# The first two blocks of an input projection computed by token halves, two of its columns moved into an earlier pool, and a third pair of split tiles

## The chip, the cores and the metric

The kernel runs on one core of one Trainium2 chip. The metric is device microseconds of that core for one execution of the whole layer. TensorE (PE) does the matrix products, VectorE (DVE), ScalarE (ACT) and GpSimd (POOL) the elementwise work, SyncE (SP) issues the transfers of the hardware queue. Each engine takes its own instructions strictly in the order in which they were put there; an instruction that waits holds up all that stand behind it on that engine.

## The reference, cut to what matters

One layer over 2048 tokens of width 1024, in 32-bit floats, with a memory of 256 tokens.

```python
u = rms_norm(h, g_mix_pre);  z = u @ w_in            # (2048, 2816)
qa, ka, va, qh, fh, ih, gh = split(z)                # 512,128,128,512,512,512,512 columns
ya = swa_with_sinks(qa, ka, va, sinks)               # 8 heads of 64, window of 128, chunks of 64
yh = hgrn2(qh, fh, ih, gh, lb, onorm)                # 4 heads of 128, gated recurrence, chunks of 64
h = h + rms_norm(concat(ya, yh) @ w_out)
m = rms_norm(mem)
h = h + rms_norm(cross_attention(rms_norm(h), m, wq, wk, wv, wo))   # 4 heads, 256 memory tokens
u = rms_norm(h);  h = h + rms_norm((silu(u @ w_gate) * (u @ w_up)) @ w_down)
```

In `hgrn2` the gate is f = lb + (1 - lb) sigmoid(fh), and the recurrence needs sums of log f over a chunk; this is the only logarithm of the layer.

## The kernel before, in words

Every product of two 32-bit numbers is made as three products of a split: a tile is written as a rounded high part and the rest (`split2`: the high part by ACT or POOL, L886 or L888, the low part by DVE as a subtraction, L889), and a matrix product is hi·hi + hi·lo + lo·hi. One such step is 128 rows by 512 columns and stands in the profile as three lines: L1017, L1018 and L1019 in `products`, L156, L157 and L158 in `mm3`.

**Stages on TensorE.** (1) `in_first`, 0 to 260 us: the input projection for the first 1024 tokens, transposed (z columns on the partitions). (2) 260 to 640 us: the same columns for the second 1024 tokens (`in_proj`, `in_cols`, one block of 128 columns at a time, weights through `wcols`), interleaved with sliding-window attention (`swa`) and the recurrence (`hgrn`) of the first half. (3) 640 to 790 us: `hgrn` of the second half, interleaved with `fold_cross`, which folds the cross-attention weights with the 256 memory tokens (products of 256 columns, weights through `wcols`). (4) 790 us to the end: the large products (w_out, cross attention, SwiGLU) as jobs of `phases`.

**Stage 1 in detail.** The order of the columns is `ORDER`: pairs of 128-column blocks, (4, 5) first, then (0, 1), (2, 3), then four pairs (10+h, 6+h) of which 10+h is a forget gate f (an "f block" below), then four pairs of the rest. `phases` runs them as one job. The contraction is cut in two halves of 512, the tokens of stage 1 in two halves of 512. For the first two blocks all eight products of the 2x2x2 cut are made (`eight`; the kinds "q" and "p"); all later ones use seven products of sums (`seven`, kind "s"), which need sums of the token quarters (`T` tiles, made from `raw` in `combined`, L915). The steps of a plain block are called 1, 2 (first token half, both halves of the contraction) and 8, 3 (second token half). In kind "q" the first token half is done in two pieces of 256 tokens.

x arrives in eight tiles of 128 tokens (`x_loads`). Each is normalised (`normed`: sum of squares by ACT at L409 into a `junk` tile, root by POOL at L102 and L104, scaling by DVE at L411), transposed by TensorE (8 transposes of 128x128, L440, in `flipped`), and evacuated: for the first token half by `first` (L457, L458: the split straight from PSUM) and `copied` (L446: the plain copy for the sums), for the second half by `later` (copy, then `split2` on POOL). The remaining eight x tiles, the second 1024 tokens, ride beside the blocks (`beside`): loaded into a `pair` tile, normalised, transposed and stored to DRAM (`un_d`).

`pair` tiles are 128 x 2 x 1024 in five buffers; they hold the z results of a block (`out`), the x tiles beside, and the scratch tile `e` in which the logarithm and the decays of an f block are made (`decays`, L629 the logarithm with a table load before and after). `part` tiles (128x512, three buffers) hold evacuated partial products (L1032) and the tanh of gates (L560). `after` finishes a block while the next is on TensorE: decays, then the two stores of z. PSUM has six banks for products and two for transposes (`psm`, `pss`).

**Around stage 2.** Stage 1 has pools of its own (`t1`, `t2`, `s1`, PSUM `ps1`). When it is over they close, and the pools of stage 2 open over the same memory: `hg` (all tiles of `swa` and `hgrn`), `wp` (three `raw` tiles, two pairs `whi`/`wlo`), `io`. `in_proj(1, u)` first makes columns 4 and 5 together, then the rest one by one. `swa_front` loads its queries `qd`, splits them (L669, L670), and makes the scores at L704 and L705; `hgrn_front` begins with the products of `qq` and `k` at L785.

**What sets the order.** The program is written once, in the order above; a scheduler then places instructions on each engine by a cost of its own, and `yield` points only say which piece is issued after which. The pools' waits are per tile: a tile that lies on an old pool's memory waits for the last use of what lay there.

## Time and profile before

| what | value |
|---|---|
| runs | 2616.89, 2620.36, 2624.73 us (median 2620.36) |
| profiled execution | 2620.68 us, its span 2619.0 us, granted TensorE clock 0.997 |
| TensorE busy | 2549.2 us, 97% |
| DVE, ACT, POOL busy | 1751.4, 1262.2, 435.6 us |
| chain that ended last | PE 75%, DMA 9%, issue 6%, DVE 5%, ACT 3% |

The span is what one execution takes between its first and last instruction in the profile; the 1.7 us around it are in the run's time alone. With TensorE busy 97% of the time, the 70 us in which it is not are the ones to look at, and besides them the microseconds in which it is busy at a lower granted clock. In a row of the timeline, the figure in brackets is how long the engine stood idle before the instruction and which instruction of which line ended that.

### The profile page before, as it was taken

To read this page: it belongs to the slowest core of one execution; us is meant where nothing else is said; L and a number is where in the kernel's file an instruction comes from. 1 tells how busy PE (TensorE), PEld (TensorE's weight loads), DVE (VectorE), ACT (ScalarE), POOL (GpSimd) and SP (SyncE) were. 2 spreads that over 40 slices of the span, in tenths; PEclk is the share of its full clock that TensorE was granted. 3 is DMA by queue.
4 is the path that set the end of the run, shared out by engine and by line. 5 is a ranking of instruction groups with operands and counts; after the bars stand their busy time and mean duration, and the time that the engine had idled before them with its cause. 6 is when DMAs were issued, how large, how long until landed. Compare 5 with 4: busy or idle time off the path is not lost.

```text
span 2619.0 us, 34847 instructions
## 1 busy us (share of the span) xinstructions
PE 2549.2 (97%) x12317; PEld 2132.4 (81%) x12317; DVE 1751.4 (67%) x2757; ACT 1262.2 (48%) x2632; POOL 435.6 (17%) x611
## 2 busy tenths in 40 slices
PE   7999999999999999999999999999999999999998
PEld 6877888888888877888878888888888888888786
DVE  7675578877545778788885655566666556564656
ACT  5463366655555566565563333344333334443543
POOL 4231344321311333212310000000000000000022
PEclk9999999999999999999999999999999999999999
DMA  5345655675877886675974622353565444566888
GB/s 185 126 147 175 190 156 164 196 234 152 246 260 265 303 289 230 216 244 186 307 252 127 205 91 79 105 193 121 177 201 193 153 136 152 201 202 184 254 213 217
DMA packets 364111, 506.03 MB, mean 193 GB/s; under 512 B 20896, under 2 KB 250272, under 8 KB 363936
## 3 DMA queue, kind: packets, MB, share of 16 engines
q1 hardware_dynamic: 357888, 481.77, 56.6%
q0 software_dynamic: 6048, 22.02, 4.7%
q8 instruction: 97, 1.59, 0.3%
q14 instruction: 78, 0.64, 0.1%
HBM read 337.00 MB, written 166.72 MB: 192 GB/s over the span
## 4 chain that ended last, share of the span: by engine, by line
PE 75%; DMA 9%; issue 6%; DVE 5%; ACT 3%; POOL 2%; SPq 1%; DVEq 0%; POOLq 0%; ACTq 0%
PE psm L1017 20%; PE psm L1018 20%; PE psm L1019 20%; PE psg L158 2%; PE psg L157 2%; PE psg L156 2%; DMA row<-y_d 1%; PE pss L1252 1%; DMA z<-in_w_out_dram 1%; DMA u_d<-row 1%; DMA h1t_d<-row 1%; SPq L75 1%; DVE T L889 1%; DMA qq<-z_d 0%; ACT T L886 0%
## 5 line engine op out<-in xcount | busy, mean ns | idle before, releaser
L1017 PE MATMUL psm<-T,S 128*128 128x512 f32 x2695 | 1044.5, 392 | 16.8 <-ACT part L1032 9.8
L1018 PE MATMUL psm<-T,S 128*128 128x512 f32 x2695 | 1049.4, 390 | 2.7 <-DVE T L889 2.6
L1019 PE MATMUL psm<-T,S 128*128 128x512 f32 x2695 | 1038.8, 390 | 4.0 <-DVE S L889 4.0
L1017 PEld LDWEIGHTS psm<-T,S 128*128 128x128 f32 x2695 | 506.7, 188 | 127.4 <-ACT part L1032 10.6
L1019 PEld LDWEIGHTS psm<-T,S 128*128 128x128 f32 x2695 | 506.6, 188 | 110.9 <-DVE S L889 5.7
L1018 PEld LDWEIGHTS psm<-T,S 128*128 128x128 f32 x2695 | 507.0, 188 | 107.8 <-DVE T L889 4.7
L889 DVE TENSOR_TENSOR S<-sraw,S 128x512 fp32r<-128x512 f32 (+1 forms) x319 | 218.2, 690 | 220.2 <-ACT S L886 204.7
L886 ACT ACTIVATE S<-sum 128x512 fp32r<-128x512 f32 (+1 forms) x314 | 188.9, 620 | 361.4 <-PE psm L1019 271.6
L889 DVE TENSOR_TENSOR S<-sum,S 128x512 fp32r<-128x512 f32 (+1 forms) x372 | 249.2, 680 | 50.6 <-ACT S L886 31.7
L1032 ACT ACTIVATE part<-psm 128x512 f32<-128x512 f32 x273 | 161.7, 597 | 247.2 <-PE psm L1019 231.7
L886 ACT ACTIVATE S<-sraw 128x512 fp32r<-128x512 f32 (+1 forms) x272 | 167.3, 616 | 109.4 <-PE psm L1019 99.6
L1378 POOL DMA_DIRECT2D row<-y_d x28 | 26.1, 932 | 1114.3 <-DVE row L1564 1021.0
L889 DVE TENSOR_TENSOR T<-row,T 128x1024 fp32r<-128x1024 f32 (+1 forms) x120 | 140.9, 1188 | 59.5 <-ACT T L886 59.0
L156 PE MATMUL psg<-u,whi 128*128 128x512 f32 x352 | 141.6, 402 | 1.7 <-POOL whi L888 1.7
L158 PE MATMUL psg<-u,wlo 128*128 128x512 f32 x352 | 140.3, 399 | 0.9 <-DVE wlo L889 0.9
L157 PE MATMUL psg<-u,whi 128*128 128x512 f32 x352 | 140.1, 398 | 0.0
L1349 ACT ACTIVATE junk<-row 128x512 f32<-128x512 f32 x160 | 99.8, 625 | 64.7 <-DVE row L1371 31.2
L886 ACT ACTIVATE T<-row 128x1024 fp32r<-128x1024 f32 x120 | 120.1, 1028 | 16.8 <-DMA row<-in_w_down_dram 7.9
L888 POOL TENSOR_SCALAR S<-sum 128x512 fp32r<-128x512 f32 x58 | 54.8, 945 | 297.0 <-PE psm L1019 224.8
L1515 DVE TENSOR_TENSOR row<-psm,part 128x512 f32<-128x512 f32 x66 | 43.7, 687 | 60.6 <-PE psm L1019 60.5
L1524 DVE TENSOR_TENSOR part<-psm,part 128x512 f32<-128x512 f32 x60 | 39.8, 688 | 62.1 <-PE psm L1019 62.0
L156 PEld LDWEIGHTS psg<-u,whi 128*128 128x128 f32 x352 | 66.7, 189 | 14.6 <-POOL whi L888 2.1
(339 smaller groups left out, 3639.3 us busy)
## 6 DMA issues: line engine op xcount, KB each, us to landing
sraw<-in_w_gate_dram SPq DMA_DIRECT2D x44, 512.0 KB, 3.9
sraw<-in_w_up_dram SPq DMA_DIRECT2D x44, 512.0 KB, 3.8
hid_d<-row SPq DMA_DIRECT2D x44, 512.0 KB, 2.6
h_d<-row SPq DMA_DIRECT2D x32, 512.0 KB, 5.2
y_d<-row SPq DMA_DIRECT2D x32, 512.0 KB, 3.4
sraw<-hid_d SPq DMA_DIRECT2D x32, 512.0 KB, 5.5
row<-y_d POOLq DMA_DIRECT2D x28, 512.0 KB, 7.9
sraw<-in_w_in_dram SPq DMA_DIRECT2D x44, 256.0 KB, 3.5
```

The lines of the kernel that those rows point to most:

```text
L156: nc.tensor.matmul(ps, ah, bh, start=(i == 0), stop=False)
L157: nc.tensor.matmul(ps, ah, bl, start=False, stop=False)
L158: nc.tensor.matmul(ps, al, bh, start=False, stop=(i == n - 1))
L886: self.nc.scalar.activation(hi, raw, AF.Copy)
L888: self.nc.gpsimd.tensor_scalar(hi, raw, 1.0, 1.0, ALU.mult, ALU.mult)
L889: self.nc.vector.tensor_tensor(lo, raw, f32(hi), ALU.subtract)
L1017: nc.tensor.matmul(ps, s[:, 0, k, :], t[:, 0, k, :], start=st, stop=False, **kw)
L1018: nc.tensor.matmul(ps, s[:, 0, k, :], t[:, 1, k, :], start=False, stop=False, **kw)
L1019: nc.tensor.matmul(ps, s[:, 1, k, :], t[:, 0, k, :], start=False, stop=sp, **kw)
L1032: nc.scalar.activation(t, ps, AF.Copy)
L1349: self.nc.scalar.activation(junk, a, AF.Square, scale=float(D) ** -0.5, accum_out=to)
L1515: nc.vector.tensor_tensor(d, a, c, ALU.add)
```

## The change

It has three parts, and it moves instructions.

*First two blocks by token halves.* The steps of blocks (4, 5) and (0, 1) are put in another order: first token half of the first block (kind "q"), first token half of the second block (kind "u"), then the second token half of the first and of the second ("v", twice). The second token half of x is so needed two half-blocks later than before. The split weights of both blocks stay in memory that long; those of the second lie in a tile of the T pool (`S_u`). 36 transposes of the identity into an unused bank stand at the start of TensorE's work, and 18 more behind the transposes of the first x tile (`turns`). The orders on ACT, DVE and POOL around the x tiles are fixed by `queued`, the sums of squares use another tile as junk, two of the x loads go behind the weights of the second block, the constants of the mixers (`mix_consts`) go last. z of these two blocks goes through 512-wide `part` tiles with a store each (eight stores of 256 KB in place of four of 512 KB). The loads of x tiles beside are issued in `after` of the block ahead.

*Two columns moved.* Columns 4 and 5 of the second 1024 tokens (96 products of 128x512, L156 to L158) are made at the end of `in_first`, with streamed S tiles and the PSUM banks of stage 1, and not by `in_cols` in stage 2. `in_proj` then begins with the third column.

*Fold.* `fold_cross` uses a third pair of split tiles, every third time; the eight split instructions that open the w_out job are issued in the last half of the `hgrn` loop and not behind it.

The start, on TensorE. `pss` and `psm` are PSUM banks, `x_0` the x tiles of the first token half, `u_00` the split of its first contraction half, `S` the split weights. Before, and then after:

```order
L440 MATMUL pss_145<-ident,x_0_111 128x128 x4
L440 MATMUL pss_150<-ident,x_0_111 128x128 x4
L440 MATMUL psm_166<-ident,x_0_111 128x128 x4
L440 MATMUL psm_171<-ident,x_0_111 128x128 x4
L440 MATMUL psm_199<-ident,x_0_111 128x128 x4
L440 MATMUL psm_204<-ident,x_0_111 128x128 x4
L1017 MATMUL psm_367<-u_00_121,S_180 128x256
```

```order
L444 MATMUL pss_132<-ident 128x128 x36
L475 MATMUL pss_179<-ident,x_0_111 128x128 x4
L475 MATMUL pss_184<-ident,x_0_111 128x128 x4
L444 MATMUL psm_193<-ident 128x128 x18
L475 MATMUL psm_231<-ident,x_0_111 128x128 x4
L475 MATMUL psm_236<-ident,x_0_111 128x128 x4
L1117 MATMUL psm_251<-u_00_120,S_219 128x256
```

The first product stood behind three x tiles and now stands behind two; 54 transposes of the identity are new. Further down, the transposes of the last three of four tiles of the second token half (`x_1`) stood together before, with the first tile beside (`pair_359`) behind them, ahead of the first product on the second half (`u_01`):

```order
L440 MATMUL pss_272<-ident,x_1_133 128x128 x4
L440 MATMUL pss_277<-ident,x_1_133 128x128 x4
L440 MATMUL pss_295<-ident,x_1_133 128x128 x4
L440 MATMUL pss_300<-ident,x_1_133 128x128 x4
L440 MATMUL pss_318<-ident,x_1_133 128x128 x4
L440 MATMUL pss_323<-ident,x_1_133 128x128 x4
L1252 MATMUL pss_794<-ident,pair_359 128x128 x4
L1252 MATMUL pss_800<-ident,pair_359 128x128 x4
L1017 MATMUL psm_479<-u_01_122,S_180 128x512
```

```order
L475 MATMUL pss_423<-ident,x_1_169 128x128 x4
L475 MATMUL pss_428<-ident,x_1_169 128x128 x4
L475 MATMUL psm_446<-ident,x_1_169 128x128 x4
L475 MATMUL psm_451<-ident,x_1_169 128x128 x4
L1117 MATMUL psm_462<-u_00_120,S_u 128x512
L1118 MATMUL psm_462<-u_00_120,S_u 128x512
```

Now two of its tiles stand ahead of the second block's first half (`S_u`), the other two 24 products further on, and the first product on `u_01` comes behind all 48 products of that half-block.

The f blocks, on ACT, around the second logarithm of stage 1 (with the semaphores that each row waits for; DMAHW are transfers). Before, `pair_1124` and `pair_1247` being z and scratch tile of that block, and then after, where these are `pair_1184` and `pair_1307`:

```order
L560 ACTIVATE th_1148<-pair_1124 128x512 [waits DVE_49]
L554 ACTIVATE pair_1124<-pair_1124 128x512 [waits DVE_49]
L629 ACT_TABLE_LOAD [waits DMAHW1_49,DMAHW0_49]
L629 ACTIVATE pair_1247<-pair_1124 128x1024 [waits Pool_49]
L409 ACTIVATE pair_1212,n_s_1606<-pair_1212 128x1024 [waits DMAHW2_49,Activation_49]
L560 ACT_TABLE_LOAD
L560 ACTIVATE th_1204<-psm_1036 128x512 [waits PE_49]
L1032 ACTIVATE part_1233<-psm_1220 128x512
```

```order
L649 ACTIVATE th_1208<-pair_1184 128x512 [waits DVE_49]
L643 ACTIVATE pair_1184<-pair_1184 128x512 [waits DVE_49]
L723 ACT_TABLE_LOAD
L723 ACTIVATE pair_1307<-pair_1184 128x1024 [waits Pool_49]
L649 ACT_TABLE_LOAD
L649 ACTIVATE th_1264<-psm_1094 128x512 [waits PE_49]
L1132 ACTIVATE part_1291<-psm_1278 128x512
```

The logarithm waited for two transfers, the stores of z of the f block ahead of it, whose buffer its scratch tile takes; now it waits for none, and the sum of squares of an x tile beside (L409) has moved from between the table loads to ahead of the block.

The passage from stage 1 to stage 2, on TensorE. `whi` is the first weight tile of the new pools. Before, and then after:

```order
L1018 MATMUL psm_2060<-T_647,S_2157 128x512
L1019 MATMUL psm_2060<-T_647,S_2157 128x512
L156 MATMUL psg_2265<-u_00_2196,whi_2253 128x512
L157 MATMUL psg_2265<-u_00_2196,whi_2253 128x512
...
L157 MATMUL psg_2378<-u_00_2196,whi_2373 128x512
L685 MATMUL pss_2452<-ident,vr_2450 128x128
L704 MATMUL pst_2462<-kh_2445,qs_0_2434 128x128
```

```order
L1118 MATMUL psm_2222<-u_10_122,S_2200 128x512
L1119 MATMUL psm_2222<-u_10_122,S_2200 128x512
L156 MATMUL psm_2295<-u_00_2258,S_2282 128x512
L157 MATMUL psm_2295<-u_00_2258,S_2282 128x512
...
L156 MATMUL psg_2443<-u_00_2258,whi_2438 128x512
...
L879 MATMUL psh_2599<-qq_2592,k_2590 128x192 x2
...
L798 MATMUL pst_2527<-kh_2510,qs_0_2499 128x128
```

The 96 products from the tiles `S_2282` on are now the last of stage 1 and read weights that were loaded in its pools; behind them come 48 products of the first new column, and then the first products of `hgrn` (L879) and `swa` (L798). Before, 96 products and a piece of a third column stood between the new pools' first tile and `swa`.

The diff, cut to its core:

```diff
-                for _ in range(2):
-                    next(cols)
+                next(cols)
...
-                for _ in self.hgrn(range(NPB, NT), "gt"):
+                for i, _ in enumerate(self.hgrn(range(NPB, NT), "gt")):
                     for _ in range(2):
                         next(fold)
-                for _ in range(8):
-                    next(phases)
+                    if 2 <= i < 10:
+                        next(phases)
...
+        turn = itertools.count()
+
+        def split_tiles():
+
+            if next(turn) % 3 < 2:
+                return self.split_tiles()
+            self._n += 1
+            return [ph.tile([P, D], F32R, tag=f"w{x}", name=f"w{x}_{self._n}") for x in ("hi", "lo")]
...
+    def turns(self, kind, n):
+
+        ps = self.bank(kind)
+        for _ in range(n):
+            self.nc.tensor.transpose(ps[:, 0:P], self.ident, self.ident)
...
-        blocks = [("q" if i == 0 else "p" if i < 2 else "s",)
-                  + self.in_block(*p, beside[i], get if i > 9 else (), None if i else lambda: x_loads(0, (2, 3)))
...
+        plain = [b[1:4] + ([],) for b in blocks[:2]]
+        blocks[:2] = ([(k, stream, out, lambda: iter(()), keep) for k, (stream, out, _, keep) in zip("qu", plain)]
+                      + [("v", lambda kind: iter([None]), out, after, keep) for _, out, after, keep in plain])
...
         next(phases)
+        self.turns("h", 36)
+        x_loads(1, (0, 1))
+        scaled(0, 0)
         b0 = first(0, "sh")
+        a0 = self.traced(ACT)
+        with self.queued(self.traced(PE)):
+            self.turns("g", 18)
+        scaled(0, 1)
+        with self.queued(self.traced(POOL), self.traced(DVE)):
+            next(phases)
         b1 = first(1, "gt")
+        a1, v1 = self.traced(ACT), self.traced(DVE)
         next(phases)
+        next(phases)
...
         for i in range(4):
-            later(i)
-        self.mix_consts()
+            if i == 2:
+                next(phases)
+                w = self.traced(PE)
+            with self.queued(*([w] if i > 1 else [])):
+                later(i, a3 if i else a2, v3)
+        self.mark()
+        with self.behind():
+            self.mix_consts()
...
+        c0 = self.ORDER[0][0] * P
+        stream = self.streamed(
+            lambda t, j: self.load(t, I["w_in"][j * 512:(j + 1) * 512, c0:c0 + 2 * P].rearrange("(k p) c -> p k c", p=P)),
+            4, "p")
+        next(stream)
+        S = list(stream)
+        z = self.pair_tile()
+        for s in range(2):
+            for i in range(2):
+                ps = self.bank("g")
+                self.mm3(ps, [((S[i + k // 4 * 2][:, 0, k % 4, :], S[i + k // 4 * 2][:, 1, k % 4, :]), u[s][k])
+                              for k in range(KT)])
+                nc.scalar.activation(z[:, i, s * 512:(s + 1) * 512], ps, AF.Copy)
+        for i in range(2):
+            self.store(self.z_d[c0 + i * P:c0 + (i + 1) * P, TB:2 * TB], z[:, i, :])
...
+                t = self.st_pool.tile([P, 512], F32, tag="part", name=f"zp_{self._n}", bufs=3)
+                nc.scalar.activation(t, a, AF.Copy)
+                self.store(self.z_d[c0:c0 + P, j * 512:(j + 1) * 512], t)
+                return
...
+            for n in beside:
+                t = self.pair_tile()
+                self.load(t[:, 0, :], self.I["x"][TB + n * P:TB + (n + 1) * P, :])
+                ahead.append((n, t))
...
-        for cols in [order[:2]] + [[c] for c in order[2:]]:
-            e1 = self.in_cols(b, u, cols, e1)
+        for c in order[2:]:
+            e1 = self.in_cols(b, u, [c], e1)
...
-    STEPS = {"s": (1, 5, 6, 3, 7, 2, 4), "p": (1, 2, 8, 3), "q": (1, 2, 8, 3)}
-    TAKES = {"s": (1,) * 7, "p": (2, 2, 0, 0), "q": (4, 0, 0, 0)}
+    STEPS = {"s": (1, 5, 6, 3, 7, 2, 4), "p": (1, 2, 8, 3), "q": (1, 2), "u": (1, 2), "v": (8, 3)}
+    TAKES = {"s": (1,) * 7, "p": (2, 2, 0, 0), "q": (4, 0), "u": (2, 2), "v": (0, 0)}
...
+        k1, k2, j = (1, 2, 0) if kind == "u" else (8, 3, 1)
+        if kind == "u":
+            keep += S[:2]
+        self.products(x, [(keep[0], T[k1], nk)], True, False)
+        self.products(y, [(keep[1], T[k1], nk)], True, False)
```

More of the change, by code (lines that the diff above doesn't have):

```diff
@@ L1111, in phases @@
         queue = sorted(uses, key=lambda k: (uses[k][0] - (5 if k[1] == 7 and jobs[k[0]][3] is None else 0), k))
-        slots = [("A", -2, i) for i in range(4)] + [("B", -1, i) for i in range(3)]
+        held = 7 if first else -1
+        slots = [("A", -2, i) for i in range(4)] + [("B", held if i == 2 else -1, i) for i in range(3)]
         T, keep = {}, [{} for _ in jobs]
@@ L1220, in phases @@
                 run = (self.seven(ready, Ready(), nk, out, addend) if kind == "s" else
-                       self.eight(ready, Ready(), nk, out, addend, kind == "q"))
+                       self.eight(ready, Ready(), nk, out) if kind == "p" else
+                       self.plain(ready, Ready(), nk, out, addend, kind))
                 for q in range(len(self.STEPS[kind])):
-                    next(run)
+                    for _ in range(1 if g or not first else 3):
+                        next(run)
+                        if first and g < 3:
+                            yield
                     self.mark()
                     upto(need[g + 2])
+                    if first and g == 1:
+                        yield
                     for _ in range(1 if kind == "s" else 2):
@@ L1234, in phases @@
                             split(g)
-                        half(g, self.row_tile)
+                        if not first or g > 1:
+                            half(g, self.row_tile)
                     g += 1
```

137 lines of the change are left out of this document (86 added, 51 removed).

## The prediction

> **What bounds the kernel now.** I read the page first, then windows of 20 us, then, where a window shows TensorE short of 20 us, the timeline of TensorE and of the engine that its row names.
>
> ```profile
> PE 2549.2 (97%) x12317; PEld 2132.4 (81%) x12317; DVE 1751.4 (67%) x2757; ACT 1262.2 (48%) x2632; POOL 435.6 (17%) x611
> ```
>
> ```profile
> core 0: us, PE busy (x) PEld busy (x) DVE busy (x) ACT busy (x) POOL busy (x), PEclk, DMA share, GB/s
> 0.00:20.00 20.00, 8.54 (x36) 7.45 (x37) 11.39 (x17) 12.86 (x24) 10.43 (x23) 1.00 0.92 303
> 20.00:40.00 20.00, 17.00 (x135) 15.62 (x133) 14.63 (x20) 12.47 (x25) 11.09 (x17) 1.00 0.33 92
> 80.00:100.00 20.00, 20.00 (x90) 16.53 (x89) 10.53 (x15) 5.65 (x11) 2.93 (x5) 1.00 0.45 149
> 140.00:160.00 20.00, 16.89 (x69) 13.81 (x70) 15.79 (x21) 11.42 (x20) 7.00 (x10) 0.91 0.46 144
> 260.00:280.00 20.00, 17.59 (x69) 14.16 (x70) 10.77 (x15) 4.05 (x6) 11.59 (x13) 0.91 0.96 246
> 760.00:780.00 20.00, 16.10 (x129) 15.48 (x130) 13.64 (x19) 9.15 (x14) 1.83 (x3) 1.00 1.03 337
> ```
>
> TensorE is the bound, and in a full window (80 to 100 us) nothing else matters. The change can only win where TensorE is idle or slow: the start, the f blocks (140), the passage (260), the fold (760). The large products after 790 us are the same as before.
>
> **The start.** TensorE, timeline, with the last step of the identity on POOL and one entry of the chain of waits (the splits of the second token half on POOL):
>
> ```profile
> 1.15 0.29 POOL masks.py:199 TENSOR_SCALAR_AFFINE_SELECT ident<-ident 128x128 f32<-128x128 f32 x1
> ```
>
> ```profile
> 35.24 3.16 POOL u L888 x4
> ```
>
> ```profile
> 8.14 1.97 PE L440 MATMUL pss<-ident,x 128*128 128x128 f32 x8 [8.14 <-DVE x L411]
> 12.44 1.97 PE L440 MATMUL psm<-ident,x 128*128 128x128 f32 x8 [2.33 <-DVE x L411]
> 15.39 1.97 PE L440 MATMUL psm<-ident,x 128*128 128x128 f32 x8 [0.98 <-DVE x L411]
> 17.01 0.78 PE L1017 MATMUL psm<-u,S 128*128 128x256 f32 x2
> 20.52 0.41 PE L1018 MATMUL psm<-u,S 128*128 128x256 f32 x1
> 20.73 0.33 PE L1019 MATMUL psm<-u,S 128*128 128x256 f32 x1
> 25.24 0.28 PE L1017 MATMUL psm<-u,S 128*128 128x256 f32 x1
> 25.36 0.28 PE L1018 MATMUL psm<-u,S 128*128 128x256 f32 x1
> 27.43 0.39 PE L1018 MATMUL psm<-u,S 128*128 128x256 f32 x1 [1.43 <-DVE u L458]
> 33.91 1.03 PE L440 MATMUL pss<-ident,x 128*128 128x128 f32 x8
> 39.97 0.98 PE L1017 MATMUL psm<-u,S 128*128 128x512 f32 x3 [0.93 <-POOL u L888]
> 43.09 0.39 PE L1019 MATMUL psm<-u,S 128*128 128x512 f32 x1
> 43.32 0.39 PE L1018 MATMUL psm<-u,S 128*128 128x512 f32 x1
> ```
>
> A product of 256 columns takes 0.21 us up to 20.73 and 0.12 us later; eight transposes 1.97 and then 1.03. TensorE runs at half speed until it has worked without a pause for some 5 us (15.39 to 20.73). A product of 512 columns takes 0.23 us. Before: first product at 17.01; the first block's first half (96 products of 256) ends at 33.9; then TensorE transposes and waits for the second token half until 39.97; then three half-blocks of 48 products of 512, 3 x 10.9 = 32.7 us. The third block starts at 72.7.
>
> After, worked out with the same rows: the identity is there at 1.44, and TensorE can start at about 1.6. 36 transposes, 22 at 0.246 and 14 at 0.129, end at 1.6 + 5.4 + 1.8 = 8.8, 0.7 us behind the first x tile; the next tile cannot be transposed before 12.4 (its DVE row is unchanged), and the 18 further transposes fill that gap. So the first product comes at 12.4 + 1.0 = 13.4, at full speed. 96 products (11.5 us), 16 transposes within (2.1) and one wait like that of 27.43 (1.4) end at 28.4. The second block's first half and the 32 transposes of the second token half (10.9 + 4.1) end at 43.4. The splits of that half on POOL (3.2 us for four, behind the last transposes at about 38) are then just ready. Two half-blocks remain, 21.8: the third block starts at 65.2, against 72.7, less 1.0 for the transposes of a tile beside that stood ahead and come later: **gain 6.5 us**. At worst the transposes of the identity stay slow throughout (36 x 0.246 = 8.9, end at 10.5) and the splits on POOL come 2 us late: 3. At best the wait of 1.4 is gone: 8.
>
> Eight z stores through three `part` buffers cost nothing as I see it: outputs come in pairs 5 to 11 us apart and a store lands within 5.4 (the row below), so three buffers last.
>
> **The f blocks.** The logarithm of the second f block on ACT, the chain ahead of it, and what TensorE waited for:
>
> ```profile
> 131.79 5.39 DMA z_d<-pair
> ```
>
> ```profile
> 137.28 1.28 ACT L629 ACT_TABLE_LOAD   x1 [3.64 <-DMA z_d<-pair]
> ```
>
> ```profile
> 119.71 0.50 PE L1017 MATMUL psm<-T,S 128*128 128x512 f32 x1 [0.55 <-ACT part L1032]
> 143.12 0.50 PE L1017 MATMUL psm<-T,S 128*128 128x512 f32 x1 [3.20 <-ACT part L1032]
> 166.04 0.50 PE L1017 MATMUL psm<-T,S 128*128 128x512 f32 x1 [1.08 <-ACT part L1032]
> ```
>
> ```profile
> 144.00:148.00 4.00, 4.00 (x12) 3.13 (x11) 3.15 (x4) 1.28 (x4) 0.70 (x3) 0.61 0.46 131
> 264.00:268.00 4.00, 4.00 (x13) 3.18 (x13) 4.00 (x3) 0.00 (x0) 3.38 (x4) 0.68 1.16 309
> ```
>
> ACT stands 3.64 us at the table load, for a store; the evacuation of a PSUM bank (L1032) is queued behind it, and TensorE waits 3.20 for that and then runs at a granted clock of 0.61: 12 products in 4 us where 17.5 fit, another 1.3. The order after shows this logarithm waiting for no transfer. What remains is the first f block's case, in which ACT's own chain of two table loads costs 0.55. So (3.20 - 0.55) + (1.08 - 0.55) + 1.3 = **4.5 us**. Bounds: 0 if the scratch tile of another block meets a late store instead, 5.5 if the rest goes too (the sum of squares no longer stands between the table loads).
>
> [...]
>
> **The passage.** TensorE and, for the cover that goes, SP's queue, the transfers from 255 to 290 us (KB each, us from issue to landing) and ACT:
>
> ```profile
> 261.47 0.50 PE L156 MATMUL psg<-u,whi 128*128 128x512 f32 x1 [1.67 <-POOL whi L888]
> 263.14 0.79 PE L158 MATMUL psg<-u,wlo 128*128 128x512 f32 x1 [0.94 <-DVE wlo L889]
> 286.69 0.31 PE L704 MATMUL pst<-kh,qs 128*128 128x128 f32 x1
> ```
>
> ```profile
> 268.03 3.00 SPq L75 DMA_DIRECT2D qd<-z_d  x2
> ```
>
> ```profile
> raw<-in_w_in_dram SPq DMA_DIRECT2D x7, 512.0 KB, 6.5
> qd<-z_d SPq DMA_DIRECT2D x6, 128.0 KB, 3.2
> ```
>
> ```profile
> 276.86 0.64 ACT L669 ACTIVATE qs<-qd 128x512 fp32r<-128x512 f32 x1 [6.17 <-DMA qd<-z_d]
> ```
>
> The first weight tile of the new pools waits for their memory, its load and its split: 1.67 + 0.94 idle and 13 products in 4 us at clock 0.68 (1.4 lost): 4.0 us. The 96 moved products (21.9 us) read weights that were loaded earlier, and the new pools' weights load and are split under them, so these 4.0 go. But the same 96 products were the cover for `swa` and `hgrn`: `qs` was ready 18 us after stage 1's end (259.8, which is 261.47 less 1.67) and TensorE reached it at 286.7, 27 us after. Now 48 products, 10.9 us, stand between the end of the moved work and L879 and L798, while the loads of `k` and `kk` wait for that end (their tiles lie on the S tiles). They have less in front of them: five of the seven weight loads of these 35 us (6.5 us each to land) come earlier, under the moved products. In front of `qd` stand eight transfers of 0.4 to 0.5 us issue, so it is issued 4 us after the end at the earliest, lands 3 to 8 us later (3.2 was the median), and its split takes ACT 0.6 and DVE about as long: ready 8.5 to 14 us after, against 11. I take a new wait of 1.3 us, nearer the lower end since the queue is empty: **gain 2.7 us**. Bounds: 4.0 with no wait, -4.5 if `qs` takes the 18 us of before (7 us of wait and 1.5 of clock).
>
> **The fold.** Rows of the groups between 756 and 782 us:
>
> ```profile
> L158 PE MATMUL psh<-mT,wlo 128*128 128x256 f32 x32 | 9.2, 287 | 1.3 <-DVE wlo L889 1.3
> L886 ACT ACTIVATE whi<-raw 128x1024 fp32r<-128x1024 f32 x8 | 8.5, 1059 | 12.2 <-PE psh L157 5.4 <-PE pss L157 3.6 <-DMA raw<-in_wv_x_dram 2.7
> L158 PE MATMUL pss<-mT,wlo 128*128 128x256 f32 x24 | 7.0, 290 | 2.8 <-DVE wlo L889 2.8
> ```
>
> TensorE waits 4.1 us for low parts, these follow ACT's high parts, and of ACT's 12.2 us of waiting 9.0 is for TensorE to leave a split tile. A third pair takes that away; the 2.7 for the weight's own transfer stay, in a stage where the transfers are full (1.03 in the window of 760). About half: **gain 2 us**, between 0 (transfers set the pace) and 4. The moved issue of the eight w_out splits I cost at nothing: on ACT they stand within five places of where they stood, under the products of `hgrn`. If they stood in front of the fold's own, ACT would hold these up by 8.5 us, as much as the eight of the row above.
>
> **The sum.** 6.5 + 4.5 + 2.7 + 2 = 15.7 us from the profiled 2620.7, which is 0.3 above the median of the runs shown: **2605 us**. With all upper bounds 2599, with all lower ones 2622.
>
> **Rivals.**
> *A, the passage turns into the new stall* (places: L798, L879). For it: the cover shrinks from 27 to 11 us, and `kk` waits for the last moved product. Against: five loads of 512 KB that were in front are gone. It decides from 12 us after the stage's end. 15.7 - 2.7 - 4.5 = 8.5 off: 2612. Chance 0.15.
> *B, the start gives little.* For it: DVE and ACT are busy 11 to 15 of 20 us there, and the splits on POOL end just when needed. Against: both engines have idle time in both windows. 3 in place of 6.5, and the f blocks 3: 2610 to 2611. Chance 0.15.
> *C, the change does not do what it says*: the store's wait moves to another f block, the start is held by late x. Gains of 0 + 2 + 2.7 + 0: 2616, no change that can be told. Chance 0.12.
> *D, slower.* The z stores of the first blocks stand on SP in one line with the loads of weights and of x beside, and a `part` buffer is free only when its store has landed. Where a load ahead of it waits for DVE's sums, the store, the evacuation on ACT and then TensorE wait. Each of the eight outputs would cost the 5.4 of a store's landing: 43 at most; it makes the kernel slower if four of them do, with the clock lost each time (4 x 6.7 = 27 against 15.7): 2632. It decides from a store held up by over 11 us. Against: DVE is idle half of the window of 80 to 100, so its sums are not late, and 11 us is twice a store's landing. Chance 0.05.
>
> **Chances and range.** Forecast 0.53. The runs of before scatter by 0.15% to either side; 0.3%, 7.9 us, is about what can be told from no change, and lies at 2612.5. Faster: the forecast, B and half of A, some of it with more gain: 0.77. Same: half of A and C: 0.17. Slower 0.06. Range: the forecast's own 2599 to 2611; with A, B and C 2597 to 2617.
>
> **What would show it.** In the profile after: transposes of the identity from about 2 us; first product at 13 to 14 and all products of 256 at 0.12; third block at 65 to 67; no wait over 1 us at the f blocks and clock 1.00 in 140:160; L156 following stage 1 without a gap; a wait at L798 or L879 below 2 us; `whi` rows of ACT in the fold without waits for L157. The prediction is wrong if the first product comes after 16, if a wait over 3 us stands at L798, or if a new one stands at L1132.

## The result, and the profile after

The changed kernel takes **2608.27 us** (median of 6 runs, 2603.4 to 2611.0) against 2621.93 for the kernel before, timed beside it (6 runs, 2616.9 to 2624.7): a ratio of **0.9946, interval 0.9933 to 0.9959**, 13.7 us less. The forecast was 2605, within 2597 to 2617, 15.7 less.

The page of the changed kernel, busy time by engine:

```profile
PE 2555.2 (98%) x12371; PEld 2138.3 (82%) x12371; DVE 1752.0 (67%) x2759; ACT 1259.7 (48%) x2633; POOL 435.2 (17%) x612
```

The 54 added matmuls are the transposes of the identity. Busy time of TensorE rose by 6.0 us and the span fell by 10.0 (2619.0 to 2609.0), so 16 us of idle time went. The windows that the prediction named, in the kernel after (columns as in the prediction: TensorE's busy time and matmuls first, its granted clock third from the end):

```profile
140.00:160.00 20.00, 16.83 (x79) 13.82 (x78) 15.46 (x20) 13.08 (x21) 7.94 (x10) 1.00 0.41 139
260.00:280.00 20.00, 20.00 (x90) 16.57 (x89) 2.15 (x7) 2.39 (x4) 6.78 (x11) 1.00 0.81 225
280.00:300.00 20.00, 17.97 (x97) 14.95 (x95) 10.73 (x34) 7.89 (x29) 5.82 (x10) 1.00 0.61 156
300.00:320.00 20.00, 16.98 (x83) 14.84 (x84) 14.79 (x43) 10.16 (x32) 3.75 (x7) 0.83 0.58 161
760.00:780.00 20.00, 17.52 (x129) 15.82 (x127) 12.81 (x19) 8.08 (x13) 1.82 (x3) 1.00 1.01 341
```

The passage's window (260) is now full. Two other windows are short, 140 and 280 to 320; both are read below.

**The start.** TensorE's timeline after, to be set beside the rows of 8.14 to 27.43 in the prediction:

```profile
8.08 1.09 PE L475 MATMUL pss<-ident,x 128*128 128x128 f32 x8 [0.97 <-DVE x L426]
11.78 1.09 PE L475 MATMUL psm<-ident,x 128*128 128x128 f32 x8 [0.64 <-DVE x L426]
13.21 0.47 PE L1117 MATMUL psm<-u,S 128*128 128x256 f32 x2 [0.34 <-ACT u L492]
14.18 0.39 PE L1118 MATMUL psm<-u,S 128*128 128x256 f32 x1 [0.50 <-DVE u L493]
27.28 1.03 PE L475 MATMUL pss<-ident,x 128*128 128x128 f32 x8
64.04 0.39 PE L1117 MATMUL psm<-u,S 128*128 128x512 f32 x1
```

The first product starts at 13.21 instead of 17.01, and eight transposes take 1.09 instead of 1.97 us from the first x tile on. The first block's first half ends at 27.28 instead of 33.91, and no wait like the 1.43 of 27.43 is left. The row of 64.04 is the first product of the third block, where the split weights change from `S_u` back to `S`. Before, it is this row:

```profile
72.79 0.39 PE L1017 MATMUL psm<-u,S 128*128 128x512 f32 x1
```

**Milestones.** Each profile gives the times of a few products of TensorE: the first product of the third block (the twelfth ahead of the first one on a sum `T`), the end of stage 1 (the first product in the new pools, less its own wait, and less the 21.9 us of moved products where they are moved), the last product of the projection, and the first large product after the fold. One profiled execution each, in us from the span's start; the names of the last three columns are those of the experiments below:

| | before | after | a_same (the changed kernel, another execution) | a_nocols | p1_only |
|---|---|---|---|---|---|
| third block | 72.8 | 64.0 | 63.9 | 64.0 | 63.6 |
| end of stage 1 | 259.8 | 248.0 | 245.5 | 246.6 | 246.2 |
| end of the projection | 643.5 | 640.1 | 633.1 | 633.7 | 634.4 |
| after the fold | 805.0 | 800.1 | 789.2 | 793.4 | 794.7 |
| span | 2619.0 | 2609.0 | 2602.0 | 2606.0 | 2608.4 |

Two executions of one program stand 10.9 us apart after the fold and 7.0 at the end. So a single profile settles a term of 2 us only where the wait itself is in its rows; sums over stages are good to several us. Of the 10 us between the spans of before and after, 5 arise behind the fold (1814 us there before, 1809 after), where the large products are the same in both kernels.

### The profile page after: what moved, and what is told of

Same layout as the page of the kernel before. It is cut to its first block, busy times and chain, and to the rows that moved or that the text cites. A ratio compares the mean times of both kernels' runs of the same rounds, so it can differ in the third digit from the quotient of the medians.

```text
span 2609.0 us, 34953 instructions
## 1 busy us (share of the span) xinstructions
PE 2555.2 (98%) x12371; PEld 2138.3 (82%) x12371; DVE 1752.0 (67%) x2759; ACT 1259.7 (48%) x2633; POOL 435.2 (17%) x612
## 4 chain that ended last, share of the span: by engine, by line
PE 79%; DMA 9%; DVE 5%; ACT 3%; issue 2%; POOL 1%; SPq 0%; DVEq 0%; POOLq 0%; ACTq 0%
PE psm L1117 22%; PE psm L1119 22%; PE psm L1118 22%; PE psg L158 1%; PE psg L157 1%; PE psg L156 1%; PE pss L1369 1%; DMA qd<-z_d 1%; DMA z<-in_w_out_dram 1%; DMA row<-y_d 1%; ACT T L980 1%; DMA raw<-in_wo_x_dram 1%; DMA u_d<-row 1%; DVE T L983 0%; DMA row<-d_s 0%
## 5 line engine op out<-in xcount | busy, mean ns | idle before, releaser
L1132 ACT ACTIVATE part<-psm 128x512 f32<-128x512 f32 x273 | 161.7, 597 | 242.8 <-PE psm L1119 220.9
L156 PE MATMUL psg<-u,whi 128*128 128x512 f32 x320 | 129.5, 405 | 0.0
L157 PE MATMUL psg<-u,whi 128*128 128x512 f32 x320 | 128.0, 400 | 0.0
L158 PE MATMUL psg<-u,wlo 128*128 128x512 f32 x320 | 127.9, 400 | 0.0
L1092 DVE TENSOR_TENSOR sum<-sraw,sraw 128x512 f32<-128x512 f32 (+1 forms) x93 | 63.8, 686 | 18.9 <-DMA sraw<-in_w_in_dram 5.7
```

What stands on the lines that cost most here:

```text
L156: nc.tensor.matmul(ps, ah, bh, start=(i == 0), stop=False)
L157: nc.tensor.matmul(ps, ah, bl, start=False, stop=False)
L158: nc.tensor.matmul(ps, al, bh, start=False, stop=(i == n - 1))
L1092: nc.vector.tensor_tensor(t, a, b, op)
L1132: nc.scalar.activation(t, ps, AF.Copy)
```

## The experiments

Each was timed in five rounds beside the kernel before; a ratio of 0.001 is 2.6 us. Three groups of four ran together: a_same, a_nocols, a_qd2 and a_cover; a_noturns, b_turns, a_nothird and a_x67 on the same chip; p1_only, b_third, best and a_noprol on another one. a_same so stood beside its own group alone.

**a_same** is the changed kernel unaltered, as the yardstick.

> The changed kernel once more, unaltered, as the measure for the three beside it. Both theories: 0.9935 to 0.996 of the kernel before (2603 to 2611 us where before is 2621).

Measured: **0.9942** (0.9927 to 0.9957), profiled span 2602.0.

**What happened at the third f block.** In the profile after, a wait of 3.17 us stands there, in a_same one of 0.77. TensorE's and ACT's timelines after:

```profile
131.89 0.50 PE L1117 MATMUL psm<-T,S 128*128 128x512 f32 x1 [0.72 <-ACT part L1132]
156.17 0.50 PE L1117 MATMUL psm<-T,S 128*128 128x512 f32 x1 [3.17 <-ACT part L1132]
```

```profile
144.22 1.06 ACT L424 ACTIVATE pair<-pair 128x1024 f32<-128x1024 f32 x1 [3.02 <-issue]
150.44 1.28 ACT L723 ACT_TABLE_LOAD   x1
153.74 1.28 ACT L649 ACT_TABLE_LOAD   x1
155.53 0.59 ACT L1132 ACTIVATE part<-psm 128x512 f32<-128x512 f32 x1
```

The same ACT row in a_same, and the load of the x tile beside (KB, us from issue to landing) first after, then in a_same:

```profile
142.14 1.06 ACT L424 ACTIVATE pair<-pair 128x1024 f32<-128x1024 f32 x1 [1.02 <-issue]
```

```profile
pair<-in_x_dram SPq DMA_DIRECT2D x1, 512.0 KB, 7.0
```

```profile
pair<-in_x_dram SPq DMA_DIRECT2D x1, 512.0 KB, 5.1
```

ACT squares an x tile (L424) ahead of the sigmoid's and the logarithm's work for this block. SP issues that load at 137.1 after and at 137.0 in a_same. In the profile after it lands 2.0 us later: the square starts 2.1 later, the two table loads and the evacuation (L1132) follow it, and TensorE waits 2.4 longer. Ten profiles that keep the load at this place fall into two groups: landing after 7.0 or 7.1 us and a wait of 3.17 or 3.27 (after, a_nothird), or landing after 4.9 to 5.2 and a wait of 0.17 to 0.77 (the other eight). Why the transfer took longer in two of them isn't shown.

**a_x67** moves this load away: x tile 6 is taken one block later, together with tile 7.

```diff
-        beside = [(), (0,), (1, 2), (3,), (4,), (5,), (6,), (7,), (), (), (), ()]
+        beside = [(), (0,), (1, 2), (3,), (4,), (5,), (), (6, 7), (), (), (), ()]
```

> The changed kernel with the seventh x tile beside loaded one block later, together with the eighth, so that no sum of squares on a freshly loaded x tile stands on ACT ahead of the decays of the third f block. Theory (the wait of 3.2 us at 153 us follows from that sum of squares, which waits 3.0 us for its tile): that wait falls below 1 us and the time is 2 to 3 us below the changed kernel. Rival (POOL's gate and the two table loads make it): it stays above 2 us.

Measured: 0.9963 (0.9950 to 0.9976). TensorE at the third and at the next f block, and the two loads:

```profile
153.90 0.50 PE L1117 MATMUL psm<-T,S 128*128 128x512 f32 x1 [0.57 <-ACT part L1132]
176.25 0.50 PE L1117 MATMUL psm<-T,S 128*128 128x512 f32 x1 [2.15 <-ACT part L1132]
```

```profile
pair<-in_x_dram SPq DMA_DIRECT2D x2, 512.0 KB, 6.9
```

The wait went along with the loads, to the block that now has two of them. That fits the late landing as the cause, and this order is not a cure for it: the gain of 2 to 3 us that was expected from it didn't come.

**a_noturns** leaves the transposes of the identity out; **b_turns** adds 36 of them to the kernel before, at the same place.

```diff
-        self.turns("h", 36)
...
-        with self.queued(self.traced(PE)):
-            self.turns("g", 18)
```

```diff
         next(phases)
+        ps = self.bank("h")
+        for _ in range(36):
+            nc.tensor.transpose(ps[:, 0:P], self.ident, self.ident)
```

> The changed kernel without the 54 transposes of the identity. If they keep the clock up: the first products of 256 columns run at 0.21 us again for some 4 to 5 us, the x transposes at 0.25; 3 to 5 us slower than the changed kernel. If the gain at the start comes from the order of the halves alone: within 1 us of it.

> The kernel before with 36 transposes of the identity at the start of TensorE's work and nothing else. Theory of the clock: the transposes of the first x tiles run at 0.13, but the idle time between the x tiles (2.3 and 1.0 us) lets the clock fall again or not; the first products come at full speed, 1 to 3 us faster than before. Theory that the second token half's arrival at 40 us sets the start: the first half-block ends earlier, but the products at 40 us do not move: within 1 us of the kernel before.

Measured: a_noturns 0.9947 (0.9932 to 0.9962), b_turns 0.9990 (0.9979 to 1.0000). TensorE in a_noturns, then in b_turns:

```profile
11.92 1.97 PE L475 MATMUL psm<-ident,x 128*128 128x128 f32 x8 [1.79 <-DVE x L426]
66.31 0.39 PE L1114 MATMUL psm<-u,S 128*128 128x512 f32 x1
```

```profile
12.58 1.19 PE L440 MATMUL psm<-ident,x 128*128 128x128 f32 x8 [3.43 <-DVE x L411]
15.57 1.97 PE L440 MATMUL psm<-ident,x 128*128 128x128 f32 x8 [1.80 <-DVE x L411]
28.78 0.39 PE L1021 MATMUL psm<-u,S 128*128 128x256 f32 x1 [3.14 <-DVE u L458]
```

Without the transposes the third block starts at 66.3 in place of 63.9 to 64.0: they are worth 2.3 us of the 8.8 there, and the order by token halves the rest. The total can't tell them from nothing (0.9947 against 0.9942). In the old order 36 of them win nothing at the start. TensorE waits for DVE longer, 3.43 us there (2.33 before) and 3.14 later (1.43 before), and loses the fast clock 0.9 us behind the first of these waits: the third tile's transposes take 1.97 us again and the products of 256 columns 0.21 each up to 20.1, and the granted clock is 0.50 from 13.44 to 20.27. The third block starts at 74.1, later than before's 72.8. So b_turns doesn't show what a clock that stays fast would win in the old order. In the new order the clock was slow at the start once too, with the transposes in place: in a_x67's profile it was 0.50 from 14.57 to 17.99, and the third block started at 65.1.

**a_nocols** puts the moved columns back into the new pools. The first pass there takes two columns again.

```diff
-                next(cols)
+                for _ in range(2):
+                    next(cols)
...
-        c0 = self.ORDER[0][0] * P
-        stream = self.streamed(
...
-        for c in order[2:]:
-            e1 = self.in_cols(b, u, [c], e1)
+        for cols in [order[:2]] + [[c] for c in order[2:]]:
+            e1 = self.in_cols(b, u, cols, e1)
```

> The changed kernel with columns 4 and 5 of the second half made in stage 2 again, as before; the rest of the change stays. Prediction as it was put: 2.7 us slower than the changed kernel. Theory from its trace (the passage lost as much as it saved): the 2.6 us of waits at the first weight tile and their slow clock are back, those at the scores (4.8 us and slow clock) are gone; within 2 us of the changed kernel, or up to 3 us faster.

Measured: 0.9949 (0.9935 to 0.9963), beside 0.9942 for a_same: no difference that can be told. What each pays at the passage, by TensorE's timeline and windows of 4 us; first a_nocols:

```profile
248.22 0.50 PE L156 MATMUL psg<-u,whi 128*128 128x512 f32 x1 [1.67 <-POOL whi L968]
250.49 0.79 PE L158 MATMUL psg<-u,wlo 128*128 128x512 f32 x1 [1.54 <-DVE wlo L969]
```

```profile
248.00:252.00 4.00, 2.25 (x6) 1.52 (x7) 2.62 (x4) 0.00 (x0) 1.21 (x2) 0.71 1.12 296
252.00:256.00 4.00, 4.00 (x11) 3.13 (x10) 1.04 (x1) 0.00 (x0) 0.00 (x0) 0.50 1.08 275
256.00:260.00 4.00, 4.00 (x18) 3.28 (x18) 1.15 (x6) 0.60 (x1) 1.95 (x4) 0.94 1.16 286
```

Then the changed kernel:

```profile
297.86 0.35 PE L798 MATMUL pst<-kh,qs 128*128 128x256 f32 x1 [0.98 <-POOL w_se L810]
303.02 0.58 PE L798 MATMUL pst<-kh,qs 128*128 128x256 f32 x1 [3.21 <-DVE qs L764]
```

```profile
300.00:304.00 4.00, 0.98 (x4) 0.98 (x5) 2.33 (x11) 1.34 (x4) 0.00 (x0) 0.69 0.46 95
304.00:308.00 4.00, 4.00 (x16) 3.71 (x15) 2.83 (x9) 1.42 (x4) 1.11 (x1) 0.50 0.66 220
308.00:312.00 4.00, 4.00 (x22) 3.35 (x21) 3.33 (x8) 1.92 (x9) 1.81 (x3) 0.96 0.66 189
```

1.67 + 1.54 = 3.2 us of waiting at the new pools, followed by clocks of 0.71, 0.50 and 0.94, were exchanged for 0.98 + 3.21 = 4.2 us some 50 us later, followed by 0.69, 0.50 and 0.96 (a_same has 0.70 and 3.09 there). The exchange is even, or a loss of an us.

**Why the scores wait.** SP's issues of the queries in the changed kernel, with the high parts on ACT and the low parts on DVE:

```profile
281.89 1.23 SPq L75 DMA_DIRECT2D qd<-z_d  x2
287.88 2.88 SPq L75 DMA_DIRECT2D qd<-z_d  x2
297.74 1.24 SPq L75 DMA_DIRECT2D qd<-z_d  x2
```

```profile
285.32 0.63 ACT L763 ACTIVATE qs<-qd 128x512 fp32r<-128x512 f32 x1 [3.76 <-DMA qd<-z_d]
295.95 0.63 ACT L763 ACTIVATE qs<-qd 128x512 fp32r<-128x512 f32 x1 [6.02 <-DMA qd<-z_d]
301.61 0.63 ACT L763 ACTIVATE qs<-qd 128x512 fp32r<-128x512 f32 x1 [2.44 <-DMA qd<-z_d]
```

```profile
281.07 0.79 DVE L764 SCALAR_TENSOR_TENSOR qs<-qd,qs 64x512 fp32r<-64x512 f32 x1 [7.63 <-ACT qs L763]
296.61 1.10 DVE L764 SCALAR_TENSOR_TENSOR qs<-qd,qs 64x512 fp32r<-64x512 f32 x1 [1.84 <-ACT qs L763]
302.27 0.69 DVE L764 SCALAR_TENSOR_TENSOR qs<-qd,qs 64x512 fp32r<-64x512 f32 x1 [1.64 <-ACT qs L763]
```

There is one buffer `qd` for both groups of heads of every window. DVE leaves it at 281.86 and SP issues the next load at 281.89; DVE leaves it at 297.71, and the next is issued at 297.74, lands, is split, and frees the scores at 303.0. In between, the load issued at 287.88 was slow: its split on ACT starts at 295.95, 8 us after the issue, where the turns beside it took 3.4 and 3.9. So loads, splits on ACT and splits on DVE follow each other in one line, and a late one delays all behind it. Before, the 96 products of the first two columns let this line get ahead; they now stand in front of it.

**a_qd2** breaks that line: in the first two windows the second group has a buffer of its own. **a_cover** leaves the line and puts one more column (10.9 us of products) in front of it.

```diff
-            qd = ph.tile([P, 4, P], F32, tag="qd", name=f"qd{n}_{g}")
+            qd = (self.io_tile("u")[:, 0:512].rearrange("p (a b) -> p a b", a=4) if g and n < 2 else
+                  ph.tile([P, 4, P], F32, tag="qd", name=f"qd{n}_{g}"))
```

```diff
-                next(cols)
+                for _ in range(2):
+                    next(cols)
                 for _ in swa:
```

> The changed kernel with a buffer of its own for the second group's queries in the first two windows of attention (four more transfers can be issued at once). Theory of lost cover: the query loads come too late because of the place at which they may start, so a second buffer takes away part only: the 3.2 us wait halves, 1 to 2 us gained. Theory of the single query buffer: the waits of 1.0 and 3.2 us go, 4 to 6 us gained.

> The changed kernel with two columns in place of one made before the first attention step of stage 2, so that 96 products and not 48 stand between the end of the moved columns and the scores. Theory of lost cover: the waits at the scores between 280 and 304 us (0.6, 1.0 and 3.2 us, and the slow clock behind them) fall below 1.5 us together, and the time is 4 to 6 us below the changed kernel. Rival (the chain of loads through one query buffer sets the pace whatever stands ahead of it): the 3.2 us wait comes back later, the time is within 2 us of the changed kernel.

Measured: a_qd2 0.9937 (0.9923 to 0.9951), a_cover 0.9941 (0.9927 to 0.9956). In both profiles the waits at the scores are gone: between 280 and 310 us a_qd2 keeps one of 0.73, a_cover none. So the single buffer, met by too little cover, is what made them. The totals moved by 1.3 us and 0.3 us from a_same, inside the intervals. a_cover's column is missing from the work further on, and in the second half TensorE waits for a load (a_cover's timeline):

```profile
638.89 1.62 PE L880 MATMUL pst<-qq,k 128*128 128x192 f32 x4 [5.33 <-DMA k<-z_d]
```

**best** takes both edits together.

> The changed kernel with both remedies at the passage: two columns ahead of the first attention step and a buffer of its own for the second group's queries in the first two windows. Theory of lost cover: no wait over 0.6 us between 270 and 310 us, as with either alone, so nothing on top of the better of the two; the 5 us wait that the earlier column left at the start of the second half's recurrence stays: 0.9935 to 0.9945. If the two waits add: 0.992.

Measured: 0.9958 (0.9943 to 0.9973), not better than the change alone. Its profile has the wait of the row above too, of 5.51 us.

**a_nothird** leaves the third pair of split tiles out; **b_third** adds it alone to the kernel before (the functions `split_tiles` and `columns` of the change).

```diff
-            if next(turn) % 3 < 2:
+            if next(turn) % 3 < 4:
                 return self.split_tiles()
```

```diff
-        raw_tile, split_tiles = self.raw_tile, self.split_tiles
+        raw_tile = self.raw_tile
+        turn = itertools.count()
...
-                wh, wl = self.wcols(w, j * P, "A")
+                wh, wl = columns(w, j * P)
```

> The changed kernel with two pairs of split tiles in the fold, as before. Prediction as it was put: 2 us slower than the changed kernel, with waits of 0.5 to 2 us for low parts back between 740 and 775 us. Rival (transfers of weights set the pace there): within 1 us.

> The kernel before with the third pair of split tiles alone. Prediction as it was put: 2 us faster, ratio 0.9992. From the run without it (0.2% slower than the changed kernel): 3 to 5 us faster, 0.998 to 0.999; the fold (last projection product to first large product) 156 to 158 us in place of 161.5. Rival (transfers set the pace): no change, 161 us.

Measured: a_nothird 0.9963 (0.9950 to 0.9977), b_third 0.9994 (0.9984 to 1.0003). Beside a_same the first would price the pair at 5.5 us, but the intervals overlap, and a_x67, which has the pair, stands at 0.9963 too. ACT's high parts in the fold, by groups of instructions from 751 to 777 us, first in the changed kernel, then without the third pair:

```profile
L980 ACT ACTIVATE whi<-raw 128x1024 fp32r<-128x1024 f32 x7 | 7.4, 1057 | 9.5 <-DMA raw<-in_wv_x_dram 8.6 <-PE pss L157 0.8
```

```profile
L980 ACT ACTIVATE whi<-raw 128x1024 fp32r<-128x1024 f32 x7 | 7.4, 1058 | 11.0 <-PE psh L157 6.1 <-DMA raw<-in_wv_x_dram 2.6 <-PE pss L157 2.2
```

ACT's wait for TensorE fell from 8.3 us to 0.8, and its wait for the weight itself rose from 2.6 to 8.6: 7.5 taken away, 6.0 put back. In the window of 760 above the transfers' share is 1.01: they set the pace, as the lower bound of the prediction had it. From the end of the projection to the end of the fold, eight profiles with the third pair (best and a_cover, which move a column across that mark, left out) take 156.1 to 161.6 us, mean 159.0, and four without it 159.1 to 162.6, mean 160.9: some 2 us, less than the scatter. b_third says 1.6 with an interval that holds zero.

**p1_only** keeps the first part of the change alone (the order by token halves with the transposes, the x tiles and the z stores): the columns, the third pair and the issue of the w_out splits are as before. **a_noprol** takes back that issue alone.

```diff
-                    if 2 <= i < 10:
-                        next(phases)
+                for _ in range(8):
+                    next(phases)
                 for _ in fold:
```

> The kernel before with the first part of the change alone (halves, transposes of the identity, x tiles, z stores of the first two blocks); columns, split tiles and the w_out splits as before. Theory from the profiles so far (stage 1 gains 13 us, some 3 of it are lost again in stage 2, whether the columns move or not): 8 to 10 us faster than before, ratio 0.9962 to 0.997, stage 1's last product near 246.4. Prediction as it was put: 11 us faster, 0.9958. If half of the gain came from the moved columns: 6 us, 0.9977.

> The changed kernel with the eight split instructions of the w_out job issued behind the recurrence, as before. Prediction as it was put (they stand within five places of where they stood): no difference to the changed kernel, 0.9935 to 0.996. If the earlier issue is what shortened the start of the fold: 2 us slower or more, above 0.996.

Measured: p1_only **0.9972** (0.9962 to 0.9982), a_noprol 0.9958 (0.9942 to 0.9975). The first part alone makes 7.3 us of the total, 4.7 to 10.0 by the interval, which leaves out the 11 of the prediction. In the table above its lead at the end of stage 1 is 13.6 us; against the profiles of b_third and b_turns, which keep the old order of the blocks and end stage 1 at 257.6 and 259.0, it is 11.4 and 12.8. Beside a_noprol and best (0.9958 both), which ran with it, the rest of the change is worth 3.7 us, inside the intervals; beside the first measurement, 0.9946, it is 6.8. The issue of the w_out splits can't be told from nothing, beside 0.9942 for a_same and 0.9946 for the first measurement.

## Why the prediction was right or wrong

**The total** was right to 2 us of 15.7, and that is in part luck. The sum put 11.0 us on the first part of the change (the start and the f blocks), for which p1_only shows 4.7 to 10.0, and 2.7 on the passage, for which no gain can be told; and it took it that what stage 1 wins arrives undiminished at the end. Of what the rest of the change brought, no single term can be told from nothing.

**The start (+6.5)** had the mechanism right and the size too small: 8.8 at the third block. The first product came at 13.2 (13.4 was worked out), and the transposes were fast from the first x tile on (1.09 us for eight). The transposes of the identity ended at 7.1 and not at 8.8, 36 in 5.62 us (6.63 in b_turns) where the sum had 7.2: the clock rose 3.1 us behind the first of them (3.9 in a_same, 5.1 in b_turns), where the sum took 5.4 from one execution. That changed nothing, since the transposes of the first x tile wait for DVE until 8.08. The baseline was right: "The third block starts at 72.7" is the row of 72.79. The step that was mis-sized is "one wait like that of 27.43 (1.4)": what came is 0.50 at 14.18, so that the first half-block ended at 27.3 in place of 28.4. From there on the sum's 36.8 us are the 36.8 of the rows, and the third block starts at 64.0 against 65.2, ahead of the 65 to 67 named. So 7.5 + 0.1 + 1.2 = 8.8; the 1.0 taken off for the transposes of the tile beside falls behind this mark, where they stand at 69.5. The second token half's splits on POOL were in time.

**The f blocks (+4.5).** The store's wait went, as the order had said, and what is left at the second f block is 0.72 (0.55 expected). But the third has 3.17 in the execution profiled. Against the profile of before, by the waits with the 1.3 of clock, the term is 3.20 + 1.3 - 0.72 + 1.08 - 3.17 = 1.7 us there, and with the 0.77 of a_same 4.1. The step that failed is "What remains is the first f block's case": with an earlier block in front, ACT's line starts at the landing of an x tile, for which ACT stands 1.02 us even in a_same, and a landing that is 2.0 us later comes out as 2.4 us more of waiting. This was a named sign of error ("if a new one stands at L1132"), seen in two of ten profiles.

The price of the old stall was one execution's too. b_third and b_turns have the old order at the f blocks; the same product there, first in b_third, then in b_turns:

```profile
142.37 0.50 PE L1033 MATMUL psm<-T,S 128*128 128x512 f32 x1 [2.23 <-ACT part L1048]
```

```profile
142.88 0.50 PE L1020 MATMUL psm<-T,S 128*128 128x512 f32 x1 [1.65 <-ACT part L1035]
```

The clock stayed at 1.00 behind both. With their waits at the second and the third f block the prediction's own sum, (3.20 - 0.55) + (1.08 - 0.55) + 1.3, gives (2.23 - 0.55) + (1.08 - 0.55) = 2.2 us and (1.65 - 0.55) + (1.88 - 0.55) = 2.4, not 4.5.

**The passage (+2.7)** is the term that was wrong. The first half of the step held: the new pools' first product follows without a gap, and the window of 260 is full, at clock 1.00. So did the first window's queries: the moved products end at 269.9, DVE has the first queries at 281.9, 12 us after (8.5 to 14 were worked out), and TensorE waits 0.58. What failed is "I take a new wait of 1.3 us": it priced the first load of `qd` and not the ones behind it, that share its buffer. The wait came one window later, 0.98 + 3.21 with a clock of 0.50 behind it, and by the rows the exchange is even or a small loss. By the totals a_nocols is 1.8 us slower than a_same, inside the intervals, which leave room for the 2.7 too. That is rival A in its mechanism, at L798 as named, 16 to 21 us after the place that the rival looked at; its price of 7.2 us against the forecast's 2.7 gain was too high by the rows, 4.2 us of waits for 3.2. The sign "a wait over 3 us at L798" was met: by two of its own signs the prediction was wrong, while its number was right.

The clock behind the waits, which the prediction priced from one execution, was 0.50 after 0.98 and 3.21 us in the changed kernel and after 1.67 and 1.54 with 0.7 us of work between in a_nocols, and 1.00 after 3.17 us that end at 156.17 in the changed kernel. The last section has such waits side by side.

**The fold (+2)** fits: some 2 us by the profiles, 1.6 by b_third, neither apart from zero. Its reason for taking half was right: transfers took over the wait.

**The w_out splits and the z stores (0)** cost nothing that a run shows; no row of the changed kernel has TensorE waiting for a `part` buffer behind a store, so rival D had no place.

**What stays open.** p1_only's lead of 11.4 to 13.6 us at the end of stage 1 is 7.3 in the total, and why isn't shown. Stage 2 may take back part of it: from the end of stage 1 to the end of the projection before took 383.7 us, b_turns 384.7 and b_third 386.9. With the new stage 1 it was 387.5 in a_same, 387.2 in a_nocols, 388.2 in p1_only and 392.1 after, but 383.5 in a_qd2 and 385.9 in a_noturns and a_noprol, so the two groups overlap. Single waits inside it change from one execution to the next: after has one of 2.75 us at 510 with a clock of 0.64 behind it, before 1.86 at 515 with 1.00. No run took these apart, and none shows which of the columns, the third pair and the issue of the w_out splits brought what the whole has over p1_only.

## What to carry to other kernels

When work is moved out from between a load and its use, follow not the first use but every later one that shares the load's buffer: a line of load, split, split through one tile needs its cover again for each turn. Where a stall goes, look for the next input of the engine that stalled and how many us it has to spare; here it had none, and a late landing brought the stall back in two of ten profiles. Price a stall from more than one execution: the one that this prediction priced at 4.5 us with its clock was worth about half of that in two others. A lead at the end of an early stage need not be the gain at the end, so time each part alone before it is credited, and profile the same program twice before a row is taken for a term.

## What the runs showed of the hardware

Waits of nearly the same length were followed by different clocks. At the third f block TensorE waits 3.17 us in the changed kernel's profile and 3.27 in a_nothird's. Windows of 4 us there, first of the changed kernel, then of a_nothird:

```profile
152.00:156.00 4.00, 1.00 (x9) 0.77 (x7) 4.00 (x5) 3.30 (x4) 0.63 (x1) 1.00 0.00 0
156.00:160.00 4.00, 3.83 (x17) 3.18 (x18) 3.64 (x6) 2.88 (x7) 2.29 (x4) 1.00 0.23 68
```

```profile
152.00:156.00 4.00, 0.73 (x8) 0.49 (x6) 4.00 (x5) 3.51 (x5) 0.45 (x2) 1.00 0.00 0
156.00:160.00 4.00, 4.00 (x11) 3.23 (x12) 3.42 (x5) 1.90 (x4) 2.25 (x4) 0.57 0.27 83
```

In the first the clock stays at 1.00; in the second it is 0.57 over the 4 us from 156, with 11 products where the first has 17. Shorter waits went both ways too: behind 2.75 us at 510 in the changed kernel the window of 512 to 516 has 0.64, and behind 1.86 at 515 in the kernel before, 2.23 in b_third and 1.65 in b_turns the clock was 1.00. So in these profiles the length of a wait alone didn't tell whether it cost the clock, and what did isn't shown here. What a wait cost in clock was read from the window behind it, and holds for that execution.

A transfer of 512 KB, issued at the same place in the order (and within 0.1 us of the same time after and in a_same), landed after 4.9 to 5.2 us in eight profiles and after 7.0 or 7.1 in two. And the stage after the fold, whose work no kernel here changes, took 1808 to 1816 us: these 8 us between profiles are more than most of the terms that were to be measured.
